# One unused 4-byte tile at the very top of SBUF: everything that grows from the top moves down by 32 bytes

## The chip, the cores and the metric

The kernel runs on 1 core of one Trainium2 chip. The metric is the device time of one execution in microseconds; lower is better. Each kernel is run several times and the median counts. The profile is one further execution taken with the hardware profiler.

## What is computed

A decoder trunk of two layers on a sequence of 1,024 tokens with 1,024 features, all in float32. Cut to what matters:

```
for i in range(2):
    sh1, sc1, g1, sh2, sc2, g2 = split(silu(c) @ ada_w[i] + ada_b[i], 6)
    h = rmsnorm(x, norm1_g[i]) * (1 + sc1) + sh1
    y = sparse_attention(h) if i == 0 else short_conv(h)     # both end in  ... @ w_out
    x = x + g1 * y
    h = rmsnorm(x, norm2_g[i]) * (1 + sc2) + sh2
    x = x + g2 * ((silu(h @ w_gate[i]) * (h @ w_up[i])) @ w_down[i])
```

`w_gate` and `w_up` are 1024 x 2816, `w_down` is 2816 x 1024, the convolution's `w_in` is 1024 x 3072. The attention scores each query against all keys with a small indexer, keeps the best 256 keys, and attends to those.

## The kernel before

**Matmuls.** A float32 product is made of three matmuls on `float32r` operands. `split` (line 506) writes an operand as a rounded part `hi` and a rest `lo`; `mm3` (line 510) issues hi x hi, hi x lo and lo x hi into one PSUM bank. In each matmul the second argument is the stationary operand (128 x 128, loaded ahead of it by a weight load, which the profile lists as PEld) and the third is the moving operand, mostly 128 x 512. The profile names a matmul as `out<-moving,stationary`, or with one name where both have the same; digits at the end of names are left out, so that `h11`, `h21` and `h22` are all `h`, and `t1` to `t4` are all `t`.

**Where weights live.** Raw weights come by DMA into the tiles `raw` (line 675: 2 buffers of 4,096 bytes per partition). `unit` (line 528) gives the pairs `whi`/`wlo` (4 buffers each, 2,048 bytes per partition) into which `split` writes. All are tiles of the pool `w` (line 497), which is opened first on the right side of SBUF: the right side is handed out from the top of SBUF downwards, the left side from the bottom upwards. Later the attention's pools `keep`, `sel`, `h` and `o` stack up below `w` on the right, and are closed again before the tail.

**Stages in time.** (1) To about 60 us: loads, modulation rows, norm. (2) To about 290 us: the attention's projections (`gemm_tile`, line 695), with the moving operand `hhi`/`hlo` in pool `h` on the right. (3) To about 650 us: attention and its output product. (4) The tail, some 1,650 us. Its products with `w_gate`, `w_up` and the convolution's `w_in` are made by `Pair` (line 1772), which computes a 2 x 2 block product with seven block products instead of eight: each `Pair` calls `product` (line 1780) seven times, each with 4 steps of 3 matmuls, the stationary operand from `unit`, the moving one from `h11`, `h21`, `h22`, `t1` to `t4` (line 1405) in left pools. There are 22 Pairs in each layer's feed-forward part and 12 in the convolution. `w_down` is done by `down_pairs` (line 1548) in seven sweeps `m1` to `m7` of 11 steps, each step with 4 x 3 matmuls. In `m1`, `m6`, `m3`, `m5` and `m7` the moving operand comes from the local `unit` (line 1576), that is from `ph11` in a left pool; in `m2` and `m4` (lines 1659 and 1666) it comes from `tk.unit`, so that moving and stationary operand are both `whi`/`wlo` on the right. `down` (line 1506), for the convolution's `w_out`, makes its first half with moving operands from `tk.unit` (8 x 8 x 3 matmuls) and its second with resident tiles `rh22`/`rt1` on the left (as many).

**What sets the order.** All operations are recorded first, and then `Plan.drain` (line 392) writes an order of instructions by estimated costs and due times: an engine runs its instructions in that order. The planner counts a float32r matmul of n columns at n x 17/38400 us (line 219). It does not look at addresses. Tiles are rings of buffers: a new tile in a ring waits for the last use of the one whose place it takes.

**Addresses.** In the compiled program of the kernel before, the right side ends at byte 229,344 of a partition, which is 32 more than a multiple of 64. All larger tiles on the right have sizes that are multiples of 64, so every one of them starts at 32 past a multiple of 64. A tile of 4 bytes takes a place of 32. Byte addresses in a partition:

| tile | side | starts at | over a multiple of 64 |
|---|---|---|---|
| `raw` | right | 204,768; 208,864 | 32 |
| `whi` | right | 212,960; 215,008; 217,056; 219,104 | 32 |
| `wlo` | right | 221,152; 223,200; 225,248; 227,296 | 32 |
| `hhi0`, `hhi1`, `hlo0`, `hlo1` (stage 2) | right | 107,744; 124,128; 74,976; 91,360 | 32 |
| `vst`, and the buffer of `qst` in `keep` | right | 184,288; 200,672 | 32 |
| `h11`, `h21`, `h22`, `t1` to `t4` (tail) | left | 52,736; 69,120; 85,504 and on, 16,384 apart | 0 |
| `ph11`, `ph21` | left | 52,736; 69,120 | 0 |
| `karena` | left | 7,232 | 0 |
| `s` (tail), `pf`, `p` (attention) | left | 196,448 and on; 56,800 and on; 40,096 and on | 32 |

A 128 x 128 block of `whi` starts 512 bytes after the one before, a 512-wide moving block 2,048 bytes, so these remainders hold for every matmul. To 512 bytes: the tail's left moving operands start at 0 over a multiple of 512, `whi` and `wlo` at 480, `hhi` and `hlo` at 224.

Of the kernel before, what the change touches and what calls it, by code (L numbers as in the profile page):

```python
# [9 lines left out]
F32 = mybir.dt.float32  # L10
# [40 lines left out]
class Store:  # L51


    def __init__(self, space):
        self.space, self.real, self.parts, self.ops = space, None, {}, []
        self.alloc, self.closed = None, False
# [394 lines left out]
P = 128  # L451
# [35 lines left out]
class Trunk:  # L487
# [3 lines left out]
    def __init__(self, plan):  # L491
        self.plan = self.nc = plan
        self.cp = Pool(plan, "const")
        self.pp = Pool(plan, "ps", space=PSUM)
        self.pa = Pool(plan, "pa", space=PSUM)
        self.pg = Pool(plan, "pg", space=PSUM)
        self.wp = Pool(plan, "w", side="right", bufs=2)


# [255 lines left out]
def trunk_kernel(tc, x, c, positions, ada_w, ada_b, norm1_g, norm2_g, attn_w_in, attn_q_norm_g,  # L755
                 attn_k_norm_g, idx_k_ln_g, idx_k_ln_b, attn_w_out, conv_w_in, conv_w,
                 conv_w_out, ffn_w_gate, ffn_w_up, ffn_w_down, rope_c, out):
    plan = Plan(tc.nc, tc)
    with ExitStack() as ctx:
        ctx.enter_context(tc.manual_schedule())  # L760
        tk = Trunk(plan)
        for p in (tk.cp, tk.pp):
            plan.open(p, ctx)
        xspill = [[plan.wrap(tc.dram_tile([P, HW], F32, name="xs%d_%d" % (i, d)), [P, HW])
                   for d in range(KT)] for i in range(NH)]
        a = Attention(tk, attn_w_in[0], attn_w_out[0], ada_w, xspill)
        a.first_norm(x, positions, lambda v: tk.setup(
            c, positions, ada_b, norm1_g, norm2_g, conv_w, attn_q_norm_g, attn_k_norm_g,
            idx_k_ln_g, idx_k_ln_b, rope_c, v, a.score[2][:, 256:384], a.score[4][:, HW:HW + 1]))
        a.project()  # L770
        a.attend()
        f = Tail(tk, ada_w, xspill)
        a.attended(f)
        f.run(ffn_w_gate, ffn_w_up, ffn_w_down, conv_w_in[0], conv_w_out[0], out)
        right, proj, left = (ctx.enter_context(ExitStack()) for _ in range(3))
        plan.open(tk.wp, ctx)
        for p, stack in ((tk.pa, left), (a.kp, left), (a.keep, right), (a.sel, right),
                         (a.hp, proj), (a.pj, proj)):
            plan.open(p, stack)
        plan.drain(a.hp, a.pj)  # L780
        proj.close()
        plan.open(a.op, right)
        plan.open(a.at, left)
        plan.drain(a.kp, a.at, tk.pa)
        left.close()
        for p in (tk.pg, *f.first):
            plan.open(p, left)
        plan.drain(a.keep, a.sel, a.op)
        right.close()
        for p in f.second:  # L790
            plan.open(p, left)
        plan.drain()
# [1083 lines left out]
```

## Time and profile before

| | |
|---|---|
| median of 3 runs | 2329.6 us (2327.48 to 2330.25) |
| the profiled execution, its own time | 2336.0 us |
| its span, first to last instruction | 2334.2 us |
| busy: matmuls (PE) / weight loads (PEld) | 2252.7 us (97%) / 1777.3 us (76%) |
| busy: VectorE (DVE) / ScalarE (ACT) / GpSimd (POOL) | 1916.6 us (82%) / 1125.7 us (48%) / 4.6 us |
| mean granted TensorE clock | 0.984 |
| DMA, mean over the span | 152 GB/s |

How to read it: a row of a group gives the engine, the operation, the tiles `out<-in`, their shapes, the count, the busy time and the mean length of one in ns, and then how long the engine was idle ahead of it and for what. The end of a matmul is modelled and matmuls overlap; so the cost of one in a full stream is the distance from one start to the next, which the timeline shows. A row of the windows view gives, for one stretch of time, each engine's busy us and its count of instructions, then the granted clock (PEclk), the DMA engines' busy share and GB/s.

### The profile page before, as it was taken

To read this page: it belongs to the slowest core of one execution; us is meant where nothing else is said; L and a number is where in the kernel's file an instruction comes from. 1 tells how busy PE (TensorE), PEld (TensorE's weight loads), DVE (VectorE), ACT (ScalarE), POOL (GpSimd) and SP (SyncE) were. 2 spreads that over 40 slices of the span, in tenths; PEclk is the share of its full clock that TensorE was granted. 3 is DMA by queue.
4 is the path that set the end of the run, shared out by engine and by line. 5 is a ranking of instruction groups with operands and counts; after the bars stand their busy time and mean duration, and the time that the engine had idled before them with its cause. 6 is when DMAs were issued, how large, how long until landed. Compare 5 with 4: busy or idle time off the path is not lost.

```text
span 2334.2 us, 32524 instructions
## 1 busy us (share of the span) xinstructions
PE 2252.7 (97%) x11435; PEld 1777.3 (76%) x11435; DVE 1916.6 (82%) x3851; ACT 1125.7 (48%) x2140; POOL 4.6 (0%) x19
## 2 busy tenths in 40 slices
PE   4999999999999989999999999999999999999999
PEld 3657875766798868888888877777888788888887
DVE  7879999687689898878787999886898976768874
ACT  5476899756755323333444662224553333334444
POOL 0000000000000000000000000000000000000000
PEclk6999999999999999999999999999999999999999
DMA  9324233443344655544983354334446432339724
GB/s 308 112 64 95 87 108 106 130 129 103 113 142 143 197 194 163 177 132 160 348 314 104 100 144 122 118 108 154 119 125 198 150 117 86 122 126 384 283 82 135
DMA packets 334189, 356.34 MB, mean 153 GB/s; under 512 B 18089, under 2 KB 218826, under 8 KB 334026
## 3 DMA queue, kind: packets, MB, share of 16 engines
q1 hardware_dynamic: 333816, 354.14, 47.1%
q8 instruction: 89, 1.46, 0.3%
q14 instruction: 74, 0.61, 0.1%
q10 hardware_dynamic: 210, 0.14, 0.0%
HBM read 282.64 MB, written 71.57 MB: 152 GB/s over the span
## 4 chain that ended last, share of the span: by engine, by line
PE 72%; DVE 12%; DMA 5%; ACT 4%; issue 2%; SPq 0%; ACTq 0%; POOLq 0%; DVEq 0%
PE ps_g L244 42%; PE ps_mm L244 22%; PE ps_sm L244 5%; DVE s L244 2%; DVE u L244 2%; DMA raw<-in_conv_w_in_dram 2%; DVE wlo L244 2%; PE ps_L L244 2%; DMA adaw<-in_ada_w_dram 2%; PE ps_o L244 2%; DVE p L244 1%; ACT p L244 1%; DVE sc L244 1%; ACT junk L244 1%; DVE adacc L244 1%
## 5 line engine op out<-in xcount | busy, mean ns | idle before, releaser
L244 ACT CAST whi<-raw 128x512 fp32r<-128x512 f32 (+1 forms) x301 | 184.5, 619 | 417.4 <-PE ps_g L244 159.6
L244 PE MATMUL ps_g<-t,whi 128*128 128x512 f32 x1184 | 373.6, 397 | 1.8 <-DVE whi L244 1.8
L244 ACT CAST whi<-s 128x512 fp32r<-128x512 f32 x276 | 171.1, 621 | 358.3 <-PE ps_g L244 136.0
L244 PE MATMUL ps_g<-h,whi 128*128 128x512 f32 x1056 | 332.7, 396 | 0.1
L244 DVE TENSOR_TENSOR wlo<-raw,whi 128x512 fp32r<-128x512 f32 (+1 forms) x314 | 214.3, 687 | 89.1 <-ACT whi L244 88.0
L244 PEld LDWEIGHTS ps_g<-t,whi 128*128 128x128 f32 x1184 | 222.3, 188 | 56.3 <-DVE whi L244 2.6
L244 PE MATMUL ps_g<-t,wlo 128*128 128x512 f32 x592 | 235.1, 397 | 2.7 <-DVE wlo L244 2.7
L244 PEld LDWEIGHTS ps_g<-h,whi 128*128 128x128 f32 x1056 | 197.5, 188 | 47.9 <-ACT whi L244 0.5
L244 PE MATMUL ps_g<-h,wlo 128*128 128x512 f32 x528 | 209.0, 396 | 0.4 <-DVE wlo L244 0.4
L244 DVE TENSOR_TENSOR wlo<-s,whi 128x512 fp32r<-128x512 f32 x276 | 189.3, 688 | 21.8 <-ACT whi L244 21.5
L244 PE MATMUL ps_mm<-t,whi 128*128 128x512 f32 x608 | 191.7, 396 | 1.7 <-ACT whi L244 1.7
L244 PE MATMUL ps_g<-ph,whi 128*128 128x512 f32 x572 | 180.3, 395 | 0.0
L244 PEld LDWEIGHTS ps_mm<-t,whi 128*128 128x128 f32 x608 | 113.8, 188 | 30.0 <-ACT whi L244 2.6
L244 PEld LDWEIGHTS ps_g<-t,wlo 128*128 128x128 f32 x592 | 111.4, 188 | 32.4 <-DVE wlo L244 5.3
L244 PEld LDWEIGHTS ps_g<-ph,whi 128*128 128x128 f32 x572 | 107.3, 188 | 26.2
L244 ACT ACTIVATE p<-p,nm,qsc 128x256 f32<-128x256 f32 (+7 forms) x128 | 112.5, 883 | 22.1 <-DVE nm L244 17.0
L244 PE MATMUL ps_mm<-t,wlo 128*128 128x512 f32 x304 | 120.3, 396 | 0.3 <-DVE wlo L244 0.3
L244 DVE SCALAR_TENSOR_TENSOR adacc<-adaw,cact,adacc 128x512 f32<-128x512 f32 x140 | 104.8, 749 | 16.8 <-DMA adaw<-in_ada_w_dram 15.8
L244 PEld LDWEIGHTS ps_g<-h,wlo 128*128 128x128 f32 x528 | 99.0, 188 | 25.1 <-DVE wlo L244 1.2
L244 ACT ACTIVATE junk<-sc,bs 128x896 bf16<-128x896 f32 (+3 forms) x124 | 109.6, 884 | 16.4 <-DVE bs L244 13.1
L244 DVE CUSTOM_DVE_ANT_0 p<-ps_L,bias 128x512 f32<-128x512 f32 (+3 forms) x192 | 100.0, 552 | 20.5 <-PE ps_mm L244 10.9
L244 DVE TENSOR_TENSOR u<-u 128x512 f32<-128x512 f32 x170 | 114.8, 688 | 1.8 <-ACT u L244 0.8
(339 smaller groups left out, 4825.1 us busy)
## 6 DMA issues: line engine op xcount, KB each, us to landing
adaw<-in_ada_w_dram SPq DMA_DIRECT2D x160, 256.0 KB
ph<-in_ffn_w_down_dram SPq DMA_DIRECT2D x66, 512.0 KB
raw<-in_ffn_w_gate_dram SPq DMA_DIRECT2D x54, 512.0 KB
raw<-in_ffn_w_up_dram SPq DMA_DIRECT2D x54, 512.0 KB
raw<-in_conv_w_in_dram SPq DMA_DIRECT2D x34, 512.0 KB
raw<-in_ffn_w_down_dram SPq DMA_DIRECT2D x44, 256.0 KB
ph<-in_ffn_w_down_dram SPq DMA_DIRECT2D x44, 256.0 KB
raw<-in_attn_w_in_dram SPq DMA_DIRECT2D x18, 512.0 KB
```

Of the source, the lines that this page charges most:

```text
L244: f(*[a.get() if isinstance(a, Ref) else a for a in args], **{k: a.get() if isinstance(a, Ref) else a for k, a in kw.items()})
```

## The change

`Trunk.__init__` makes one more pool on the right side, `top`, with a single float32 tile of one element per partition; no instruction reads or writes it. `trunk_kernel` opens it just ahead of `w`. It takes the highest 32 bytes of the right side, and all that is handed out below it starts 32 bytes lower: `raw`, `whi`, `wlo`, and in the attention `keep`, `sel`, `h` and `o`. The left side stays where it is. The list of instructions and their order stay the same.

```diff
         self.pg = Pool(plan, "pg", space=PSUM)
+        self.top = Pool(plan, "top", side="right")
+        self.top.tile([P, 1], F32, name="top")
         self.wp = Pool(plan, "w", side="right", bufs=2)
...
-        plan.open(tk.wp, ctx)
+        for p in (tk.top, tk.wp):
+            plan.open(p, ctx)
```

## The prediction, made before the changed kernel ran

> **What bounds the kernel now.** I read the page first, for the busy times and the chain that ended last.
>
> ```profile
> span 2334.2 us, 32524 instructions
> PE 2252.7 (97%) x11435; PEld 1777.3 (76%) x11435; DVE 1916.6 (82%) x3851; ACT 1125.7 (48%) x2140; POOL 4.6 (0%) x19
> PE 72%; DVE 12%; DMA 5%; ACT 4%; issue 2%; SPq 0%; ACTq 0%; POOLq 0%; DVEq 0%
> ```
>
> TensorE is busy for 97% of the span and holds 72% of the chain. The profiled execution took 2336.0 us, 6.4 us over the median of 2329.6; I work in the profiled execution's times and take the difference off the median. Since the change removes and adds no instruction, its only lever is the time that an instruction takes at another address. So I looked for instructions of one kind that already run at different addresses. For 128x512 matmuls the timeline gives the distance from one start to the next. Here are three undisturbed stretches, first and last row of each.
>
> ```profile
> 267.83 0.39 PE L244 MATMUL ps_mm<-hhi,wlo 128*128 128x512 f32 x1
> ...
> 273.95 0.39 PE L244 MATMUL ps_mm<-hhi,wlo 128*128 128x512 f32 x1
> ```
>
> ```profile
> 1289.74 0.39 PE L244 MATMUL ps_g<-whi 128*128 128x512 f32 x1
> ...
> 1309.91 0.39 PE L244 MATMUL ps_mm<-whi,wlo 128*128 128x512 f32 x1
> ```
>
> ```profile
> 1949.83 0.40 PE L244 MATMUL ps_g<-t,whi 128*128 128x512 f32 x1
> ...
> 1969.89 0.40 PE L244 MATMUL ps_g<-h,whi 128*128 128x512 f32 x1
> ```
>
> The first stretch, in the attention's projections, has 27 steps from first to last start: 6.12 us / 27 = 0.2267 us. The second, in sweep `m2` of `down_pairs`, has 89: 20.17 / 89 = 0.2266 us. The third, in the second layer's Pairs, has 86: 20.06 / 86 = 0.2333 us. Same engine, same shape, same types, and 6.6 ns apart. The granted clock is not the reason, as the windows of the second and third stretch show:
>
> ```profile
> core 0: us, PE busy (x) PEld busy (x) DVE busy (x) ACT busy (x) POOL busy (x), PEclk, DMA share, GB/s
> 1290.00:1310.00 20.00, 20.00 (x90) 16.57 (x89) 16.75 (x29) 8.35 (x15) 0.00 (x0) 1.00 0.27 93
> 1950.00:1970.00 20.00, 20.00 (x87) 16.06 (x87) 14.88 (x24) 6.67 (x12) 0.00 (x0) 1.00 0.44 146
> ```
>
> PEclk is 1.00 in both, PE is busy throughout, and the faster stretch is the one with more DVE and ACT work beside it. What sets them apart is where operands start. The stationary operand starts at 32 over a multiple of 64 bytes in all three. The moving one starts at 32 as well in the first two (`hhi`; `whi` and `wlo`), at 0 in the third (`h` and `t` on the left). So a matmul whose two operands start at the same remainder over 64 takes 226.6 ns, one whose operands differ by 32 takes 233.3 ns. Most of the kernel is of the second kind, and the change moves only the stationary operands there: to remainder 0, where the moving ones are.
>
> **The tail's matmuls: the gain.** The slow kind, counted from the code: 56 Pairs (22 + 12 + 22) x 7 products x 4 x 3 = 4,704; five sweeps of `down_pairs` x 11 x 4 x 3 x 2 layers = 1,320; the second half of `down`, 8 x 8 x 3 = 192. Together 6,216. The count agrees with the groups: 4 of 7 products move a `t` tile, with `whi` stationary in 2 of 3 matmuls, 56 x 4 x 4 x 2 = 1,792, which is 1184 + 608 of
>
> ```profile
> L244 PE MATMUL ps_g<-t,whi 128*128 128x512 f32 x1184 | 373.6, 397 | 1.8 <-DVE whi L244 1.8
> L244 PE MATMUL ps_mm<-t,whi 128*128 128x512 f32 x608 | 191.7, 396 | 1.7 <-ACT whi L244 1.7
> L244 PE MATMUL ps_g<-ph,whi 128*128 128x512 f32 x572 | 180.3, 395 | 0.0
> L244 PE MATMUL ps_g<-wlo,whi 128*128 128x512 f32 x150 | 58.4, 389 | 0.0
> ```
>
> The modelled lengths say the same: 395 to 397 ns where the moving tile is on the left, 389 where it is `wlo` or `whi`. If all 6,216 fall from 233.3 to 226.6 ns the tail's TensorE time falls by 6,216 x 6.6 ns = 41.0 us.
>
> **Who would be late next.** The gain shows only as far as the other engines keep up. The rows of the three densest stretches:
>
> ```profile
> 680.00:1000.00 320.00, 313.74 (x1348) 249.35 (x1347) 286.21 (x474) 118.26 (x201) 0.00 (x0) 0.99 0.56 175
> 1342.00:1581.00 239.00, 236.49 (x1016) 188.88 (x1015) 216.94 (x375) 83.47 (x142) 0.00 (x0) 1.00 0.42 122
> 1626.00:1900.00 274.00, 272.68 (x1179) 218.36 (x1178) 236.15 (x393) 112.37 (x193) 0.00 (x0) 1.00 0.47 143
> ```
>
> DVE is busy for 89%, 91% and 86% there; with 2.8% less matmul time, 92%, 93% and 89%. It stays under TensorE, but not by much, and it already makes TensorE idle for 6.3 + 2.5 + 1.3 = 10.1 us in these rows. I let that idle time grow by half, 5 us, as an estimate between nothing (as in stretches where PE is busy without a gap) and three times as much, 15 us (DVE orders its work in sequence, so one late transfer for `adaw` holds the splits queued behind it, and TensorE waits for those). DMA is used at 0.42 to 0.56 here and has room. That leaves 41 - 5 = 36 us, between 41 - 15 = 26 and, with nothing given back, 41.
>
> **What moves without effect.** In the projections and in `m2`, `m4` and the first half of `down`, both operands move by 32 together; the remainders stay equal, and the time stays at 226.6 ns. In the attention, `qst` (every second block) and `vst` move while `karena` and `pf` stay, so that the remainders of `pf` and `vst`, equal now, will differ. These are plain float32 matmuls, and there remainders don't show: `karena` against `karena` is 0 and 0, `karena` against `qst` 0 and 32, with equal shortest and median lengths:
>
> ```profile
> L244 PE MATMUL ps_L<-karena,qst x384: 269/589/792, 312.5 to 621.7; 64*128 64x512 f32 x96, 64*128 64x128 f32 x32, 64*128 64x256 f32 x32, 64*128 64x384 f32 x32
> ```
>
> ```profile
> L244 PE MATMUL ps_L<-karena x160: 269/589/1217, 97.2 to 185.0; 64*128 64x512 f32 x96, 64*128 64x384 f32 x32, 64*128 64x128 f32 x16, 64*128 64x256 f32 x16
> L244 PE MATMUL ps_o<-pf,vst 128*64 128x128 f32 x1152 | 77.5, 279 | 2.2 <-ACT on L244 1.9 <-DVE bs L244 0.2
> ```
>
> Were that wrong for `ps_o`, its 1,152 at 6.6 ns would cost 7.6 us, half of it if the two of a pair run side by side; I take 0 and keep 4 us of it for the range. ScalarE and VectorE don't see remainders either. A cast from `raw` to `whi` (32 to 32) and one from `v` to `t` (mostly 0 to 0) take the same:
>
> ```profile
> L244 ACT CAST whi<-raw x301: 426/621/692, 41.9 to 2320.9; 128x512 fp32r<-128x512 f32 x150, 128x288 fp32r<-128x288 f32 x1
> L244 ACT CAST t<-v x36: 602/621/627, 696.6 to 1728.1; 128x512 fp32r<-128x512 f32 x36
> ```
>
> So they cost 0. For DMA the nearest rows are the loads at the start, into the right side, and the densest stretch of loads into `ph` on the left:
>
> ```profile
> 0.00:60.00 60.00, 27.89 (x106) 19.19 (x107) 46.87 (x95) 29.31 (x48) 1.76 (x13) 0.63 0.91 311
> 2100.00:2180.00 80.00, 80.00 (x345) 64.28 (x344) 63.72 (x102) 34.80 (x60) 0.00 (x0) 1.00 1.02 379
> ```
>
> 311 GB/s at a share of 0.91 is 342 at a full share, against 372: at most 8% of 60 us, a gain of 5 us at the start if all of it came from remainders. The start's transfers are also cut smaller, and that explains a difference as well, so I take 0. At 80 us with the DMA engines full, the faster matmuls would ask for data 2 us sooner; the PE row shows no gap there, and I keep this within the 5 us given back.
>
> Sum: 2336.0 - 36 = 2300 us for a profiled execution, and 2329.6 - 36 = 2293.6, rounded to 2294, for the median. Own range: from a gain of 41 plus 1 for rounding, 2287, to one of 26 - 4 = 22, 2308.
>
> **The rivals.**
>
> *The moving operand alone decides, and 0 is the slow remainder.* The three stretches fit this as well: the slow one differs in its moving operand. No matmul of before has the stationary operand at remainder 0 for long, so the trace can't exclude it. Then the tail stays at 233.3 ns, and what is fast now becomes slow, because `hhi`, `hlo` and `whi`, `wlo` as moving operands go to remainder 0: 192 x 3 + 16 x 3 = 624 in the projections, by
>
> ```profile
> L244 PE MATMUL ps_mm<-hhi,wlo 128*128 128x512 f32 x192 | 77.8, 407 | 0.0
> L244 PE MATMUL ps_mm<-hhi,wlo 128*72 128x512 f32 x16 | 7.0, 440 | 0.0
> ```
>
> and 528 + 192 = 720 in `m2`, `m4` and `down`. 1,344 x 6.6 ns = 8.9 us, so 2338.5: slower. It decides from the first long run of projection matmuls on. What speaks against it is that an operand on the rounder address would have to be the slower one, whatever the other does. The Trainium skill speaks for it: by "SBUF — State Buffer", section "Who interferes with whom", TensorE has one read port for the moving operand and another for weights, independent of each other, and it never waits on anyone. By that, the weights' place could not matter, and 2338.5 would be the time; whether this chip follows it no run shows yet. Chance 0.11.
>
> *Nothing changes.* The two operands may have to agree to more than 64 bytes. The fast pairs of before agree to 256 (`hhi` at 224 and `whi` at 480 over a multiple of 512). After the change, `whi` starts at 448 and the tail's moving operands at 0: equal over 64, but 64 apart over 128 or more. Then the tail stays at 233.3 ns and the rest moves together, 2329.6. The same time would come if the tile took no place, which the order of opening excludes. By another rule of the same page of the Trainium skill, "Specifications", SBUF is read in lines of 16 bytes; a shift of 32 would then leave each operand as it lies to its lines, and nothing would change. But starts at 0 and 32 are both on such lines, and the rows differ by 6.6 ns, so the trace disagrees. Chance 0.13.
>
> *The gain is half eaten.* TensorE gets faster, but in the three dense stretches DVE becomes the bound and they stay as long as they are. They hold 313.74 + 236.49 + 272.68 = 823 us of matmuls, 2.8% of which is 23 us: the gain is 41 - 23 = 18 us, 2312. For it, DVE's 91% and the chain's 12% in DVE; against it, that PE waits so little now. Chance 0.10.
>
> **How the numbers follow.** The forecast has what is left, 0.66. Faster by over 0.2% (4.7 us, about what a measurement of this kernel can tell from no change): 0.66 + 0.10 = 0.76; within: 0.13; slower: 0.11. The range takes in the forecast and the half-eaten gain, 0.76, and must reach the unchanged time to hold 8 in 10: 2287 to 2331. The likeliest case's own range is 2287 to 2308.
>
> **What would show it.** Right: in the changed kernel's tail a `t,whi` stretch steps at 0.2266 us with PEclk at 1.00, `m2` and the projections still at 0.2266, and PE's busy time is some 41 us less. The moving-operand rival shows as 0.2333 in the projections and in `m2`; the rival of no change as 0.2333 in the Pairs alone; the half-eaten gain as 0.2266 with some 20 us more of waits of PE for `wlo` and `whi`. I'm wrong if the tail's step stays, or if steps fall and the span does not.

## The result and the profile after

| | before | after |
|---|---|---|
| median, measured side by side | 2329.93 us (4 runs, 2327.48 to 2338.4) | 2308.97 us (4 runs, 2307.38 to 2311.05) |
| ratio, 95% interval | | 0.9905, 0.9882 to 0.9927 |
| profiled execution, its own time / span | 2336.0 / 2334.2 us | 2307.38 / 2305.7 us |

The kernel is 21.0 us faster, 0.9%, where the forecast was 36 us. That is just outside the likeliest case's own range (2287 to 2308) and inside the whole one (2287 to 2331). The page of the changed kernel, the same three lines as for before:

```profile
span 2305.7 us, 32524 instructions
PE 2224.8 (96%) x11435; PEld 1777.7 (77%) x11435; DVE 1912.0 (83%) x3851; ACT 1125.6 (49%) x2140; POOL 4.7 (0%) x19
PE 70%; DVE 13%; DMA 7%; ACT 3%; issue 2%; SPq 0%; ACTq 0%; POOLq 0%; DVEq 0%
```

PE's busy time fell by 27.9 us where the forecast said some 41; the weight loads, VectorE, ScalarE and every count stand as they were. Now the timeline of the changed kernel at the prediction's three stretches: the same matmuls by their place in PE's order, first and last row of each.

```profile
266.70 0.39 PE L244 MATMUL ps_mm<-hhi,wlo 128*128 128x512 f32 x1
...
272.82 0.39 PE L244 MATMUL ps_mm<-hhi,wlo 128*128 128x512 f32 x1
...
1274.09 0.39 PE L244 MATMUL ps_g<-whi 128*128 128x512 f32 x1
...
1294.26 0.39 PE L244 MATMUL ps_mm<-whi,wlo 128*128 128x512 f32 x1
...
1927.06 0.39 PE L244 MATMUL ps_g<-t,whi 128*128 128x512 f32 x1
...
1946.74 0.39 PE L244 MATMUL ps_g<-h,whi 128*128 128x512 f32 x1
```

Projections: 6.12 us / 27 steps = 226.7 ns, as before. `m2`: 20.17 / 89 = 226.6 ns, as before. The tail's 86 steps: 19.68 us instead of 20.06, which is 228.8 ns instead of 233.3. So the tail became faster by 4.4 ns a step and not by 6.6: it stopped short of what the projections and `m2` reach. The steps are not alike: the trace's starts, in ns, go 229, 232, 226 and again, 687 for three. In before they go 231, 234, 235, which is 700, and in `m2` 227, 227, 226.

The groups show it as well. Their modelled length falls from 395 to 397 ns to 392 to 394, and not to the 389 of `wlo,whi`, which stays:

```profile
L244 PE MATMUL ps_g<-t,whi 128*128 128x512 f32 x1184 | 369.6, 394 | 2.7 <-DVE whi L244 2.2 <-ACT whi L244 0.6
L244 PE MATMUL ps_mm<-t,whi 128*128 128x512 f32 x608 | 189.5, 392 | 1.6 <-ACT whi L244 1.6
L244 PE MATMUL ps_g<-ph,whi 128*128 128x512 f32 x572 | 178.2, 392 | 0.0
L244 PE MATMUL ps_g<-wlo,whi 128*128 128x512 f32 x150 | 58.4, 389 | 0.0
```

The windows of the changed kernel, at the prediction's three dense stretches (the same matmuls), then the tail's stretch and the start:

```profile
core 0: us, PE busy (x) PEld busy (x) DVE busy (x) ACT busy (x) POOL busy (x), PEclk, DMA share, GB/s
676.00:989.60 313.60, 308.02 (x1348) 249.78 (x1347) 284.07 (x473) 117.77 (x201) 0.00 (x0) 0.99 0.57 178
1326.30:1563.70 237.40, 233.35 (x1016) 188.91 (x1015) 216.36 (x375) 83.16 (x142) 0.00 (x0) 1.00 0.42 122
1608.70:1878.10 269.40, 267.77 (x1179) 218.47 (x1178) 235.49 (x392) 112.55 (x191) 0.00 (x0) 1.00 0.48 146
...
1927.00:1947.00 20.00, 20.00 (x89) 16.38 (x89) 14.94 (x25) 6.82 (x12) 0.00 (x0) 1.00 0.44 147
...
0.00:60.00 60.00, 27.41 (x111) 18.46 (x112) 47.54 (x97) 29.24 (x48) 1.77 (x13) 0.74 0.90 313
```

The dense stretches shrink from 320.0 + 239.0 + 274.0 = 833.0 us to 820.4, while DVE's work in them is the same. PE's idle time there is 5.6 + 4.1 + 1.6 = 11.3 us, against 10.1 before. The clock in the tail is 1.00 as before. The start moves 313 GB/s at a share of 0.90, as before 311 at 0.91.

Where the time went, step by step over the whole tail: the left tiles (`t`, `h`, `ph`, `rt`, `rh`) are the moving operand of 6,216 matmuls of 512 columns, as counted. All but some 60 to 70 of their steps, which wait for something, are under 242 ns. These plain steps average 233.32 ns before (6,154 of them) and 228.96 after (6,145): 4.36 ns x 6,150 = 26.8 us less. In the remaining ones, the time above 227 ns is 17.5 us in before's trace and 19.7 in after's.

### The profile page after: what moved, and what is told of

Its sections match the earlier page's. It is cut to its first block, busy times and chain, and to the rows that moved or that the text cites. A ratio compares the mean times of both kernels' runs of the same rounds, so it can differ in the third digit from the quotient of the medians.

```text
span 2305.7 us, 32524 instructions
## 1 busy us (share of the span) xinstructions
PE 2224.8 (96%) x11435; PEld 1777.7 (77%) x11435; DVE 1912.0 (83%) x3851; ACT 1125.6 (49%) x2140; POOL 4.7 (0%) x19
## 4 chain that ended last, share of the span: by engine, by line
PE 70%; DVE 13%; DMA 7%; ACT 3%; issue 2%; SPq 0%; ACTq 0%; POOLq 0%; DVEq 0%
PE ps_g L244 40%; PE ps_mm L244 22%; PE ps_sm L244 5%; DVE u L244 2%; DMA raw<-in_conv_w_in_dram 2%; DVE s L244 2%; DVE wlo L244 2%; PE ps_L L244 2%; PE ps_o L244 2%; DMA adaw<-in_ada_w_dram 1%; DVE p L244 1%; ACT p L244 1%; DVE sc L244 1%; DVE v L244 1%; DVE adacc L244 1%
## 5 line engine op out<-in xcount | busy, mean ns | idle before, releaser
L244 PE MATMUL ps_g<-t,wlo 128*128 128x512 f32 x592 | 232.5, 393 | 1.6 <-DVE wlo L244 1.6
L244 PEld LDWEIGHTS ps_mm<-t,whi 128*128 128x128 f32 x608 | 114.0, 188 | 26.9 <-ACT whi L244 2.5
```

The costliest lines, as they stand in the source:

```text
L244: f(*[a.get() if isinstance(a, Ref) else a for a in args], **{k: a.get() if isinstance(a, Ref) else a for k, a in kw.items()})
```

## The experiments

**Theories.** From the traces of before and after, the theory was: a step's time depends on the distance between the start of the moving and that of the stationary operand, over a span longer than 64 bytes, probably 256. The distance is counted as moving minus stationary, over 512 bytes, with 512 added where it is negative. In the tail it was 0 - 480, that is 32, before and is 0 - 448, that is 64, after; in the projections it is 224 - 480, that is 256, in `m2` 0. Rivals: the moving operand's own start decides; the stationary one's own start decides; equal remainders over 64 are enough and something else holds the tail at 228.9; the place on the right side or its size does it, whatever the distance. All kernels compute the whole of the reference. For the larger top tiles 1 KB was given up elsewhere to make room, of the scratch for DMA descriptors (5,120 to 4,096 bytes; the tail's left tiles lie 1,024 lower then, the same over 512). `e5_scratch_only` has that edit alone. The same 86 tail steps are quoted from each timeline, first and last row. Runs 2 to 12 are one execution each; before took a median of 2333.34 us (7 runs) on the occasion of runs 1 to 8 and 2338.82 (one run) on that of runs 9 to 12.

**1. `e1_shift224`: distance 256.**

```diff
-        self.top.tile([P, 1], F32, name="top")
+        self.top.tile([P, 56], F32, name="top")
...
-                    dynamic_dma_scratch_size=5120)
+                    dynamic_dma_scratch_size=4096)
```

> The unused tile is 224 bytes instead of 4, so weights start 256 over a multiple of 512, as the projections' operands lie to each other; 1,024 bytes that GpSimd's DMA scratch area held at the bottom are given up for it, so the left side moves down by 1,024 and keeps its remainders over 512. Theory 1 (the distance of the moving operand's start from the stationary one's, taken over 256 bytes, decides; 64 bytes leave a third of the cost): every tail matmul steps at 226.6 ns, the whole takes 2329.9 - 41 + 5 = 2290 to 2300. Rival A (equal remainders over 64 are enough and what is left at 229 ns has another cause, such as waits for weights): steps of 229.0 ns on average as with 32 bytes, 2309. Rival B (the absolute start decides): 229.0 as well.

Measured: 2290.36 us (4 runs, 2286.16 to 2290.99), ratio to before 0.9804, interval 0.9785 to 0.9824. The page's busy line and the tail's stretch:

```profile
PE 2210.6 (97%) x11435; PEld 1779.0 (78%) x11435; DVE 1910.4 (83%) x3851; ACT 1125.8 (49%) x2140; POOL 4.6 (0%) x19
```

```profile
1912.90 0.39 PE L244 MATMUL ps_g<-t,whi 128*128 128x512 f32 x1
...
1932.39 0.39 PE L244 MATMUL ps_g<-h,whi 128*128 128x512 f32 x1
```

19.49 us / 86 = 226.6 ns: what the prediction had expected of 32 bytes. PE's busy time is 42 us less than before's, and the time 43 us less. So the rate of `m2` can be had in the tail, and VectorE does not stand in the way.

**2. `e2_shift64`: distance 96.**

```diff
-        self.top.tile([P, 1], F32, name="top")
+        self.top.tile([P, 16], F32, name="top")
```

> The unused tile is 64 bytes: weights start 96 bytes below a multiple of 512 (416 over one), at 32 over a multiple of 64, the tail's moving operands at 0. Theory 1 (distance over 256): a distance of 96, which has not been seen; between 226.6 and 233.3 ns. Rival A (equal remainders over 64 decide): unequal again, 233.3 ns and 2330. Rival B (absolute start of the weights over 64): as before the change, 233.3 ns.

Measured: 2327.18 us, and in the tail

```profile
1940.97 0.39 PE L244 MATMUL ps_g<-t,whi 128*128 128x512 f32 x1
...
1961.04 0.39 PE L244 MATMUL ps_g<-h,whi 128*128 128x512 f32 x1
```

20.07 / 86 = 233.4 ns: another 32 bytes give everything back, at the slow end of what theory 1 allowed. Since the remainder over 64 is 32 again, this run alone does not tell 64 from 256.

**3. `e3_shift128`: distance 160.**

```diff
-        self.top.tile([P, 1], F32, name="top")
+        self.top.tile([P, 32], F32, name="top")
```

> The unused tile is 128 bytes: weights start 160 bytes below a multiple of 512, at 32 over a multiple of 64. Theory 1: a distance of 160, the first one over half of 256; if the cost falls with distance, 0 at 32 bytes short of it, 226.6 ns and about 2293. Rival A: unequal remainders over 64, 233.3 ns, 2330. Rival B: 233.3 ns, 2330.

Measured: 2333.89 us, and in the tail

```profile
1945.57 0.40 PE L244 MATMUL ps_g<-t,whi 128*128 128x512 f32 x1
...
1965.71 0.40 PE L244 MATMUL ps_g<-h,whi 128*128 128x512 f32 x1
```

20.14 / 86 = 234.2 ns, slightly more than before's. The cost does not fall with the distance, as theory 1's "if" had it; 233.3 ns, which the rivals named, is nearer.

**4. `e4_left32`: before's right side, and the left side 32 bytes up instead.** Distance 64 again, with both operands at 32 over a multiple of 64.

```diff
+        self.cp.tile([P, 8], F32, name="pad")
```

(on before: a 32-byte tile at the bottom of the first left pool, no top tile)

> The kernel before, without the unused tile on the right, but with one of 32 bytes at the bottom of the left side: weights stay at 32 over a multiple of 64, the tail's moving operands go up to 32. The distance is 64, as in the changed kernel, and both starts are 32 past a multiple of 64. Theory 1: as the changed kernel, steps of 229.0 ns on average in the repeating 229, 232, 226, about 2309. Rival B (absolute starts at multiples of 64 brought the gain): 233.3 ns, 2330. If two starts at 32 are good as such, as in the sweeps m2 and m4: 226.6 ns, 2293.

Measured: 2320.2 us, and by the timeline

```profile
275.76 0.39 PE L244 MATMUL ps_mm<-hlo,whi 128*128 128x512 f32 x1
...
1940.19 0.39 PE L244 MATMUL ps_g<-t,whi 128*128 128x512 f32 x1
...
1959.87 0.39 PE L244 MATMUL ps_g<-h,whi 128*128 128x512 f32 x1
```

19.68 / 86 = 228.8 ns, with after's pattern 229, 232, 226. Moving the other operand the other way gives the same step: neither operand's own start decides, their distance does. The whole is 11 us longer than after, and 9 us of that are there long before the tail: the matmul behind the first row quoted, the first of the projections' stretch, starts at 275.98 us, in after at 266.70. `e11_shift256` is late at that place too, at 275.59 us beside 269.54 in `e5_scratch_only`, with other addresses. The windows show a lower granted clock in both: from 140 to 150 us it is 0.50 there, and 1.00 in before, after and `e5_scratch_only`; over 120 to 160 us it is 0.79 in both and 0.91 in the three others. 40 us x 0.12 makes 4.8 us at full clock, an estimate, and so about half of the 9 us. Whether the addresses have a part in that is not shown; the tail's steps don't hang on it.

**5. `e5_scratch_only`: the smaller scratch alone, on before.** Distance 32, as in before.

```diff
-                    dynamic_dma_scratch_size=5120)
+                    dynamic_dma_scratch_size=4096)
```

> The kernel before, with nothing changed but the 1,024 bytes of GpSimd's DMA scratch given up, as in the run with 224 bytes: the left side moves down by 1,024, a multiple of 512. Theory 1 (only the distance of the two operands' starts over 256 bytes counts): tail steps of 233.3 ns, about 2330. Rival (the smaller scratch area itself brought a part of the gain with 224 bytes): under 2325.

Measured: 2330.76 us, and in the tail

```profile
1943.97 0.40 PE L244 MATMUL ps_g<-t,whi 128*128 128x512 f32 x1
...
1964.03 0.40 PE L244 MATMUL ps_g<-h,whi 128*128 128x512 f32 x1
```

20.06 / 86 = 233.3 ns, as before: the smaller scratch has no part in the tail's step in `e1_shift224`.

**6. `e6_shift96`: distance 128.**

```diff
-        self.top.tile([P, 1], F32, name="top")
+        self.top.tile([P, 24], F32, name="top")
```

> The unused tile is 96 bytes: weights at 384 over a multiple of 512, the tail's moving operands at 0; a distance of 128, a multiple of 64. Theory 1 (distance over 256; multiples of 64 cheaper than odd multiples of 32): between 226.7 and 233.3 ns; if a distance of 64 and one of 128 are alike, 229.0 and about 2309. Rival (starts that agree over 128 are enough): 226.7 ns and about 2290.

Measured: 2323.97 us, and in the tail

```profile
1939.01 0.40 PE L244 MATMUL ps_g<-t,whi 128*128 128x512 f32 x1
...
1959.00 0.39 PE L244 MATMUL ps_g<-h,whi 128*128 128x512 f32 x1
```

19.99 / 86 = 232.4 ns. Here the two starts are a multiple of 128 bytes apart, and the step is nearly as slow as before's: agreement over 64, or over 128, is not enough.

**7. `e7_shift160`: distance 192.**

```diff
-        self.top.tile([P, 1], F32, name="top")
+        self.top.tile([P, 40], F32, name="top")
...
-                    dynamic_dma_scratch_size=5120)
+                    dynamic_dma_scratch_size=4096)
```

> The unused tile is 160 bytes, with the scratch given up: weights at 320 over a multiple of 512, a distance of 192, three times 64. Theory 1: as with a distance of 64, 229.0 ns and about 2309. Rival (a shorter way round to 256 counts, so that 192 is as 64; or the cost grows with the distance): 229.0 for the first, over 229 for the second.

Measured: 2331.74 us; the same 86 steps took 20.07 us, 233.3 ns each. So theory 1's second half fell, that any multiple of 64 is cheap: 64 is, 128 and 192 are not. The shorter way round fell too, since 192 is 64 short of 256 and costs as much as 32.

**8. `e8_gap224`: only `wlo` stays at distance 32, `whi` goes to 256.** No top tile; a 224-byte tile between the two. `whi` is stationary in two matmuls of three, `wlo` in the third.

```diff
-        return [self.wp.tile([P, HW], F32R, name="w" + v, tag="w" + v, bufs=self.UNITS)
-                for v in ("hi", "lo")]
+        hi = self.wp.tile([P, HW], F32R, name="whi", tag="whi", bufs=self.UNITS)
+        if not hasattr(self, "gap"):
+            self.gap = self.wp.tile([P, 56], F32, name="gap", tag="gap", bufs=1)
+        return [hi, self.wp.tile([P, HW], F32R, name="wlo", tag="wlo", bufs=self.UNITS)]
...
-                    dynamic_dma_scratch_size=5120)
+                    dynamic_dma_scratch_size=4096)
```

> No unused tile at the top; one of 224 bytes lies between the tiles whi and wlo of the weights, scratch given up: whi lies 256 from the tail's moving operands, wlo 32, as before the change. In three matmuls the stationary operand is whi, whi, wlo. Theory 1a (the weight load that runs during a matmul, the next one's, meets its moving operand): of three steps only the one that follows the second matmul, during which wlo is loaded, is long: 226.7, 233.3, 226.7, mean 228.9, about 2309. Theory 1b (a matmul's own stationary operand counts): the step that follows the third is long. Theory 1c (nothing to do with weight loads): all three alike.

Measured: 2314.72 us; the tail and `m2` by the timeline:

```profile
1277.31 0.40 PE L244 MATMUL ps_g<-whi 128*128 128x512 f32 x1
...
1297.96 0.39 PE L244 MATMUL ps_mm<-whi,wlo 128*128 128x512 f32 x1
...
1929.79 0.39 PE L244 MATMUL ps_g<-t,whi 128*128 128x512 f32 x1
...
1949.66 0.39 PE L244 MATMUL ps_g<-h,whi 128*128 128x512 f32 x1
```

The tail: 19.87 / 86 = 231.0 ns. If a step paid only for its own stationary operand, or only for the one loaded behind it, one step in three would pay 6.6 ns: 228.9. By kinds, over all plain steps with these distances (under 242 ns, the tail and the projections): 229.1 ns where this and the next stationary operand are both `whi`, 231.2 where `wlo` is next, 233.9 where `wlo` is this one's. None stays at 226.7. `m2` slows as well, 20.65 / 89 = 232.0 ns, because `whi` and `wlo` are no longer a multiple of 256 apart, and there too in every kind of step: 231.6 ns even where moving, stationary and next stationary operand are all `whi`.

**9. `e9_gap32`: the reverse, `wlo` at 256 and `whi` at 288.** The 224-byte top tile and a 32-byte tile between `whi` and `wlo`.

```diff
-        self.top.tile([P, 1], F32, name="top")
+        self.top.tile([P, 56], F32, name="top")
...
+            self.gap = self.wp.tile([P, 8], F32, name="gap", tag="gap", bufs=1)
...
-                    dynamic_dma_scratch_size=5120)
+                    dynamic_dma_scratch_size=4096)
```

(the tile between as in `e8_gap224`)

> The unused tile of 224 bytes on top and one of 32 between whi and wlo, scratch given up: wlo lies 256 from the tail's moving operands, whi 288, which is 32 over 256; the mirror image of the run with a gap of 224, whose three steps had means of 229.1 (own whi, next whi), 231.2 (own whi, next wlo) and 233.9 ns (own wlo, next whi). If a matmul's own stationary operand at a distance of 32 lengthens its step: the steps after the two whi matmuls near 233, the one after wlo near 229. If the next one's weight load does: long after the first and the third. If any change of the distance between loads costs: about as with the gap of 224, mean 231.4.

Measured: 2331.27 us; `m2` and the tail:

```profile
1281.95 0.40 PE L244 MATMUL ps_g<-whi 128*128 128x512 f32 x1
...
1302.60 0.40 PE L244 MATMUL ps_mm<-whi,wlo 128*128 128x512 f32 x1
...
1944.47 0.40 PE L244 MATMUL ps_g<-t,whi 128*128 128x512 f32 x1
...
1964.53 0.40 PE L244 MATMUL ps_g<-h,whi 128*128 128x512 f32 x1
```

The tail is back at 20.06 / 86 = 233.3 ns although a third of its stationary operands are now placed well. By kinds: 235.6 ns with `whi` now and next, 233.3 with `wlo` next, 230.9 with `wlo` now. Three of them are 19.8 ns over 3 x 226.67, just as in before. So neither "its own" nor "the next" fits, nor the third expectation, a mean of 231.4 as with the other gap; and the cost is not paid by single matmuls: a step is slowed by its neighbours' operands too. `m2` is at 20.65 / 89 = 232.0 ns again. In these two runs a step's time is thus not set by its own pair alone; what the runs leave standing is the rule for a stream whose stationary operands all lie at one distance.

**10. `e10_shift480`: distance 512, which is 0.**

```diff
-        self.top.tile([P, 1], F32, name="top")
+        self.top.tile([P, 120], F32, name="top")
...
-                    dynamic_dma_scratch_size=5120)
+                    dynamic_dma_scratch_size=4096)
```

> The unused tile is 480 bytes, scratch given up: weights and the tail's moving operands both start at a multiple of 512. Theory 1 (distance over 256): as with 224 bytes, 227.0 ns and 2286 to 2291. Rival (a distance of 256 over 512 is the good one): over 229.

Measured: 2287.78 us. The tail's stretch, and the windows of the three dense stretches (the same matmuls as above):

```profile
1910.05 0.39 PE L244 MATMUL ps_g<-t,whi 128*128 128x512 f32 x1
...
1929.55 0.39 PE L244 MATMUL ps_g<-h,whi 128*128 128x512 f32 x1
```

```profile
core 0: us, PE busy (x) PEld busy (x) DVE busy (x) ACT busy (x) POOL busy (x), PEclk, DMA share, GB/s
675.60:984.90 309.30, 304.16 (x1347) 248.37 (x1346) 284.76 (x474) 117.95 (x200) 0.00 (x0) 1.00 0.57 181
1319.50:1551.70 232.20, 230.22 (x1015) 189.25 (x1014) 215.64 (x375) 83.37 (x142) 0.00 (x0) 1.00 0.41 125
1596.90:1861.50 264.60, 264.60 (x1178) 218.59 (x1177) 235.07 (x393) 112.39 (x192) 0.00 (x0) 1.00 0.48 148
```

19.50 / 86 = 226.7 ns: distances 0 and 256 are alike. The dense stretches take 806.1 us, 26.9 less than before's; DVE is busy there for 92%, 93% and 89%, the very shares that the prediction worked out, and PE waits for 5.1 + 2.0 + 0.0 = 7.1 us, less than before's 10.1.

**11. `e11_shift256`: distance 288, which is 32 over 256.**

```diff
-        self.top.tile([P, 1], F32, name="top")
+        self.top.tile([P, 64], F32, name="top")
...
-                    dynamic_dma_scratch_size=5120)
+                    dynamic_dma_scratch_size=4096)
```

> The unused tile is 256 bytes, scratch given up: weights at 224 over a multiple of 512, a distance of 288, which is 32 over 256, as in the kernel before. Theory 1: 233.3 ns with the same 231, 234, 235 between starts, about 2330, though the tile is 32 bytes larger than the one that gave 2290. Rival (farther from the top is better): at most 2290.

Measured: 2339.06 us, beside 2338.82 for before on that occasion, and in the tail

```profile
1952.69 0.39 PE L244 MATMUL ps_g<-t,whi 128*128 128x512 f32 x1
...
1972.76 0.39 PE L244 MATMUL ps_g<-h,whi 128*128 128x512 f32 x1
```

20.07 / 86 = 233.4 ns, before's step with before's pattern 231, 234, 235. With `e10_shift480` this says that the distance counts over 256 bytes, and that a bigger tile on top is not better by itself: 224 bytes help, 256 do not, 480 do.

**12. `e12_after_again`: after itself once more.** No edit.

> The changed kernel as it is, once more. Its tail steps were 228.9 ns on average; over 242 ns its long steps add up to 38.7 us against 32.1 in the run with the smaller scratch alone and 32.6 in the one with 224 bytes. If these 6 us of waits come with the change: again 37 to 40 us and 2307 to 2311. If they differ from run to run: 31 to 36 us and 2302 to 2306.

Measured: 2311.06 us; the 86 steps in 19.68 us, 228.8 ns; the steps that wait are 22.8 us over 227 ns, against 19.7 in the first trace. That is how far this term moves between two executions of one kernel. By the expectation's measure (all 128x512 steps, what is over 242 ns) this run has about 42 us, just above the 37 to 40 of the first case and far from the 31 to 36 of the second: the longer waits come with the change.

**All distances.** Plain steps of the tail (under 242 ns), over all of it. In `e6_shift96` the pattern itself reaches 241 to 243 ns; with the 122 steps just above 242, its mean is 232.5.

| distance over 256 | kernel | mean step, ns |
|---|---|---|
| 0 | `e1_shift224`, `e10_shift480` | 226.9, 226.9 |
| 32 | before, `e5_scratch_only`, `e11_shift256` | 233.3, 233.3, 233.3 |
| 64 | after, `e12_after_again`, `e4_left32` | 229.0, 229.0, 229.0 |
| 96 | `e2_shift64` | 233.4 |
| 128 | `e6_shift96` | 232.3 |
| 160 | `e3_shift128` | 234.3 |
| 192 | `e7_shift160` | 233.3 |

## Why the prediction was partly right

**Right: the lever.** The time fell because the tail's step depends on the distance of its two operands; of the change's other effects the traces show only the longer waits told below. `e4_left32` and the pair `e10_shift480`, `e11_shift256` show it by moving one operand at a time.

**Wrong: the size of the term.** The step that failed is the first half of the sentence "So a matmul whose two operands start at the same remainder over 64 takes 226.6 ns", and with it "6,216 x 6.6 ns = 41.0 us". The count was exact. The 6.6 ns belong to agreement over 256, as runs 1, 6 and 10 show; a distance of 64 brings 4.36 ns, 26.8 us. The rows of before could not give that number: all its tail matmuls have distance 32, all its others 0 or 256. But the prediction had noticed in its second rival that the fast pairs agree to 256 and after's would not, and gave that 0.13; the premise of that rival was right and its price wrong, since at 64 the tail is neither as fast as at 0 nor as slow as at 32. That it lies between the two, nearer to 0, while 128 is nearly as slow as 32, could not be read from the trace of before. That the result lies inside the whole range says little for the prediction: the range reached up to 2331 to take in the rivals, and the likeliest case's own range ended at 2308.

**The 5 us given back.** The traces show the steps that wait 17.5 us over 227 ns in before, 13.4 in `e5_scratch_only` and 16.0 in `e11_shift256`, mean 15.6; 19.7, 22.8 and 23.6 in after, `e12_after_again` and `e4_left32`, mean 22.0. That is 6.4 us more, close to the 5 taken. With -26.8 it makes -20.4 us, beside a measured -21.0. But the size came out by luck: the prediction's reason for it, VectorE near its limit, does not hold: at the full rate of distance 0, where VectorE is pressed harder, the same term is 13.6 (`e1_shift224`) and 13.2 (`e10_shift480`). The waits themselves do end with VectorE: one step behind a `ps_g<-t,whi` matmul of the convolution, which waits for `wlo`, takes 778, 870 and 847 ns in the three kernels with distance 32, 1208, 1404 and 1359 in after, `e4_left32` and `e12_after_again`, and 595 and 719 in the two with distance 0. What makes these waits longer at distance 64 alone is not settled; each kind has a scatter of some 4 us.

**The two profiles differ by 28.6 us, the medians by 21.0.** Before's profiled execution was 6.4 us over its median. From the first row quoted of the projections to that of `m2` it took 1289.74 - 267.83 = 1021.9 us, after 1274.09 - 266.70 = 1007.4; `e5_scratch_only`, with before's steps throughout, took 1015.6. So some 6 us of the fall in that part are the scatter of one execution and not the change.

**Costs set at 0.** `ps_o` has 1,152 matmuls in 78.0 us of modelled length (77.5 before), though `pf` and `vst` now differ in their remainders; the casts of `raw` to `whi` take 620 ns (619) and the subtractions 685 (687); the start's transfers run at the same rate. All as taken.

**The rivals.** *The moving operand alone decides*: fell. The projections and `m2` kept 226.7 ns with their moving operand at remainder 0, and the tail got faster. The Trainium skill, "SBUF — State Buffer", section "Who interferes with whom", gives TensorE two independent read ports, one for the moving operand and one for the weight load. By that the place of the weights could not matter; the runs disagree, with 226.9 to 234.3 ns for one and the same stream of matmuls, by that place alone. *Nothing changes*: fell, see above. *The gain is half eaten*: its 2312 us lies nearest to the result, by luck, for its mechanism fell. The dense stretches did get shorter, by 12.6 us in after and by 26.9 in `e10_shift480`, and PE waits there for 11.3 and 7.1 us, beside 10.1 before.

**Open.** What collides is not shown. Runs 8 and 9 show that the stationary operands of the matmuls around one take part and that the delay spreads over neighbouring steps; they don't show where in the chip it arises, nor why 64 costs a third of what 32 and 128 cost. A matmul and a weight load by themselves, outside the kernel, were not measured.

The best version of these is the unused top tile of 224 or 480 bytes, with 1 KB less scratch: 2290.36 us (0.9804, interval 0.9785 to 0.9824), or 2287.78 in a single run.

## What to carry to other kernels

Where 128x512 `float32r` matmuls, each with its own weight load, follow each other without a gap, place stationary and moving operands a multiple of 256 bytes apart; an unused tile ahead of a pool is enough for that, and it was worth 2.0% here. To predict such a change, list the addresses of operands beside the start-to-start step of each class of matmul, and carry over a step only to pairs that agree to as many bytes as the measured pair does; any agreement short of that is an unknown, and not even bounded by the two known prices: here it came to 229.0 to 234.3 ns, beside 226.6 and 233.3. Compare the same run of matmuls, by its place in the order, across kernels: 86 steps settled here in each run what whole times did not, which differ by 4 to 11 us between executions of one kernel.

## What the runs showed of the hardware

- The 128x512 `float32r` step follows the distance of the operands' starts over 256 bytes, and not evenly: 226.9 ns at 0, 229.0 at 64, 232.3 to 234.3 at 32, 96, 128, 160 and 192. It was unexpected that 64 is better than 128.
- The cost comes in patterns over three steps (229, 232, 226 at 64; 231, 234, 235 at 32) and passes to neighbours whose own operands are well placed (231.6 ns in `e8_gap224` for `whi` by `whi` with `whi` next, where after has 227.4).
- The place on the right side, the scratch's size, and remainders of VectorE's, ScalarE's and the plain float32 matmuls' operands made no difference that the traces show.
